# Four small moves in a one-layer hybrid decoder step: a weight cast, a norm's sum, the last pair's products, a row tile's store

## The chip, the cores and the metric

One core of one Trainium2 chip runs one decoder layer on a prompt of 512 tokens and eight samples of four tokens. The metric is the device time of one execution in microseconds (us); of several executions the median is taken. TensorE is called PE below, its weight loads PEld; VectorE is DVE, ScalarE is ACT, GpSimd is POOL, and SyncE, which only issues DMAs here, is SP.

## What is computed

The reference, cut to its frame (all in float32, model width 1024, 4096 feed-forward columns each for gate and value):

```python
def _layer(x, ...):
    m, ... = _mixer(_rmsnorm(x, norm_mix_pre), ...)      # recurrence + windowed attention, then @ w_out
    x = x + _rmsnorm(m, norm_mix_post)
    f, ffn_state = _conv_ffn(_rmsnorm(x, norm_ffn_pre), ffn_prev, w_up, ffn_conv_w, ffn_conv_b, w_down)
    x = x + _rmsnorm(f, norm_ffn_post)

def _mixer(h, ...):
    xr, q, k, v, g_lru, g_attn = split(h @ w_in)
    lru_out = rg_lru(causal_conv(xr, width 4))           # 8 block-diagonal gate groups
    attn = window_attention(q, k, v, window 128, 8 heads, 2 kv heads, sinks, relative bias)
    return (sigmoid(g_lru) * (lru_out @ w_lru_o) + sigmoid(g_attn) * (attn @ w_attn_o)) @ w_out

def _conv_ffn(h, prev, w_up, conv_w, conv_b, w_down):
    val, gate = split(causal_conv(h @ w_up, width 3))
    return (gelu(gate) * val) @ w_down
```

Outputs are the 512 prompt rows y_p, the 32 sample rows y_s, and the states of both groups.

## The kernel before

All 544 tokens (512 and 32) are handled together, with the model dimension on the partitions and tokens along the free side, in two halves of 272 (or 256 and 288 in the down projection). A float32 factor is split into a high part H (a rounded copy in the type fp32r, made by ACT or DVE: `wh_...`, `hH`, `fH`, `b21H`) and a low part L (the factor less its high part, a DVE or POOL subtraction: `wl_...`, `hL`, `fL`, `b21L`). Each product of factors is three matmuls: H by H, H by L and L by H, summed in PSUM.

The program runs through these stages: the first tiles of x are transposed and multiplied by a first weight; the input projection (`pmin`); recurrence and attention; their output projections (`pmlo`, `pmao`); w_out (`pmout`); the post norm, the residual x1 and the second pre norm; the up projection, in which pairs of columns (a gate column block and a value block, p_ = 0 to 31) are formed by seven products named a11, a12, p2, p3, p1, p4, a22 on sums and differences of four quarter operands b11, b21, b12, b22; tap (the width-3 convolution) and glu (gelu(gate) * value, split into fH and fL); the down projection (`pmdn`) in groups of four pairs, the last group (weights `wh_dl`, `wl_dl`) being kept to the end; the post norm; and the rows sent out.

PE runs in the order in which the program writes its instructions, in the whole kernel. ACT and DVE run in written order as well in the parts that the change touches, and SP in the last part. Work beside the products is written between them in steps: generators yield a number of steps, `later(k, f, ...)` puts f behind the next k steps. So a number in such a place sets where on PE, ACT and DVE an instruction stands.

Four places matter.

The start. `hsplit(k, ...)` splits one turned tile of x: ACT writes hH, DVE writes hL (`hL`, line 177). The loop of line 485 runs over z = 0, 1 (two halves of the model dimension) and k, four tiles each. Between them a weight half is cast to its high part by DVE (`wsplit_hi(..., eng=dve)`, line 285), and POOL subtracts for its low part (line 290). The matmuls `pm_first` follow, then the transposes of the other half of x (`ps_ta`, line 473).

The second norm. The function `norm_chain(a, ...)` sums the squares of x1 for half a. On DVE the partial squares are added into `accx`; then

```python
        yield NORM_TICKS[a]
        with tc.high_priority(offset=HP):
            r = stats(acc2, nch, f"f{a}")
            yield YS[a]
            dg = diag(r, n, f"f{a}")
        yield YB[a]
        with tc.high_priority(offset=HP):
            rep = spread(dg, n, f"f{a}")
```

`stats` is six small matmuls with ones (`pst_f`, half 1 at 446 us), then ACT's square root and DVE's Newton steps (`nst_f`); `diag` and `spread` put the result on all partitions by PE (`rep_f`). From there DVE makes the normalized tiles `h2t` and the operands b12 and b22. Meanwhile PE forms products of the operands b11 and b21, whose results are `pq_...` and are copied out to `ec`; their weights are `wh_e`, `wl_e`.

The last pair. For p_ = 31, a chain of tap and glu steps is laid between the last products (lines 1680 to 1685). glu 1 finishes `z` on DVE, glu 2 makes fH on ACT, glu 3 makes fL on DVE. On the same engines stand the splits of the last down weights (`wl_dl`) and the sums `ft += pmdn` which empty the down projection's PSUM tiles.

The tail. `rows_t(i)` turns row tile i back to rows (eight transposes `pyo`, two ACT copies into `yo`) and returns a function that issues its store. Row tiles 2 and 3 and the 32 sample rows leave like this; tiles 0 and 1 leave as `xtok`. `ends(z)` forms the last products of tile 1 (`pend`), `ends_square` their squares for the norm (ACT), `ends_gain` a DVE product, and `tokens_out` the result and its store.

Of the kernel before, what the change touches and what calls it, by code (L numbers as in the profile page):

```python
# [17 lines left out]
P = 128  # L18
# [35 lines left out]
APART = ()  # L54
DN_BUFS = 2
SUMS = (4, 3)
NORM_TICKS = (3.5, 1)
YS = (0.5, 0.5)
HP = 150
NSTART = (1, 0.5)  # L60
# [63 lines left out]
def hawk_step(ctx, tc, I, O):  # L124
    nc = tc.nc
    act, dve, pool, pe = nc.scalar, nc.vector, nc.gpsimd, nc.tensor
# [22 lines left out]
    def RAW(name):  # L149
        return rp.tile([P, D], F32, tag="raw", name=name)  # L150
# [4 lines left out]
    def PX(name):  # L155
        return psx.tile([P, 512], F32, tag="aux", name=name)
# [63 lines left out]
    ident = keep.tile([P, P], F32, name="ident")  # L220
# [50 lines left out]
    def wsplit_hi(un, eng=None):  # L271
        i, u = un // 2, un % 2
        hl = []
        for x in "hl":
            if order[i] in in_slots:
                t_ = S(f"w{x}{u}_{wname(i)}", F32R)[:, 0:512]
                t_ = t_.rearrange("p (k n) -> p k n", k=4)
            else:
                t_ = wp.tile([P, 4, P], F32R, tag="w", name=f"w{x}{u}_{wname(i)}")
            hl.append(t_)  # L280
        raw = wraw[i][:, 4 * u:4 * u + 4, :]
        if eng is None:
            act.activation(hl[0], raw, AF.Copy)  # L283
        else:
            eng.tensor_copy(hl[0], raw)
        wunits[un] = hl
        return raw, hl

    def wsplit_lo(raw, hl, eng=None):
        (eng or dve).tensor_tensor(out=hl[1], in0=raw, in1=f32(hl[0]), op=ALU.subtract)  # L290
# [78 lines left out]
    TOK = [(i * P, P, xp[i * P:(i + 1) * P, :]) for i in range(4)] + [(SEQ, NS, xs)]  # L369
# [82 lines left out]
    def hsplit(k, a, ps):  # L452
        g = pv[:, G_PRE + k:G_PRE + k + 1]
        act.activation(h.get(k, a, 0), ps, AF.Copy, scale=g)
        stt(h.get(k, a, 1), ps, g, f32(h.get(k, a, 0)), ALU.mult, ALU.subtract)
# [7 lines left out]
    def first_mm(k, i0, i1, start=False, stop=False):  # L463
        mm(first_ps[:, :256], wunits[k // 4][i0][:, k % 4, :], h.get(k, 0, i1), start, stop)
# [3 lines left out]
    def turn_a(z):  # L468
        for k in range(4 * z, 4 * z + 4):
            if not z:  # L470
                ps_ta.append(PX(f"ps_ta{k}"))
            for q in range(2):
                pe.transpose(turned_a(k)[:, q * P:(q + 1) * P], xtile(q, k), ident)

    def turned_a(k):
        return ps_ta[k % 4][:, k // 4 * 256:k // 4 * 256 + 256]

    def first_low(z):
        for k in range(4 * z, 4 * z + 4):
            first_mm(k, 1, 0, stop=k == KD - 1)  # L480
# [4 lines left out]
    for z in range(2):  # L485
        for k in range(4 * z, 4 * z + 4):
            hsplit(k, 0, turned_a(k))
            if k % 4 == 1 - z:
                raw, hl = wsplit_hi((u0, u1)[z], eng=dve)
                wsplit_lo(raw, hl, eng=pool)  # L490
        for k in range(4 * z, 4 * z + 4):
            first_mm(k, 0, 0, start=k == 0)
            if z and k > 4:
                first_mm(k - 1, 0, 1)
        if z == 0:
            turn_a(1)
            for k in range(4):
                first_mm(k, 0, 1)
            first_low(0)
# [733 lines left out]
    def norm_chain(a, acc):  # L1233
# [8 lines left out]
        with tc.high_priority(offset=HP):  # L1242
# [12 lines left out]
            for g in range(6 if a else 0):  # L1255
# [15 lines left out]
                yield 0.5  # L1271
        yield NORM_TICKS[a]
        with tc.high_priority(offset=HP):
# [246 lines left out]
    def product(ps, ws, nm, start, stop):  # L1520
        for k in range(4):
            wh, wl = (ws[j][:, k, :] for j in range(2))
            xh, xl = operand(nm, k, 0), operand(nm, k, 1)
            for i, (w, x) in enumerate(((wh, xh), (wh, xl), (wl, xh))):
                pe.matmul(ps[:, :HN], w, x, start=start and k == 0 and i == 0, stop=stop and k == 3 and i == 2,  # L1525
                          skip_group_check=True)
# [111 lines left out]
    def pair(p_, nm):  # L1638

        jv, jg = p_, 32 + p_  # L1640
        ps, e = pst.setdefault(p_, {}), e_.setdefault(p_, {})
        bank = {"a11": "x", "a12": "z", "p2": "x", "p3": "y", "p1": "x", "p4": "w" if p_ in apart else "x",
                "a22": "y"}[nm]
        start = bank not in ps
        if start:
            ps[bank] = PX(f"pu{bank}_{p_}")
        product(ps[bank], usplit["s", p_, nm], XOF[nm], start, nm in ("a12", "p4", "a22") or bank == "x" and nm == "p1" and p_ in apart)
        z = ps[bank][:, :HN]

        def taken(nm_):  # L1650

            e[nm_] = EP(f"{nm_}_{p_}")
            act.copy(e[nm_], z)  # L1653

        def u4_c22():
            taken("u4")
            ug = utile(jg)
            for o, y in zip(halves2(ug, ps["y"]), halves2(ug, e["u4"])):
                sub(o[0], o[1], y[1])

        def c11():
            add(utile(jv)[:, 2:2 + HN], e["e1"], z)

        def c12():
            if p_ in apart:
                for o, y in zip(halves2(ut[jv], z), halves2(ut[jv], e["u4"])):
                    add(o[0], y[1], o[1])
            else:
                for o in halves2(ut[jv], z):
                    act.copy(*o)  # L1670
            states(jg if p_ < 31 else jv)

        def c21():
            sub(ut[jg][:, 2:2 + HN], z, e["u2"])
            states(jv if p_ < 31 else jg)

        if nm in ("a11", "a12", "p2", "p1", "p4", "a22"):
            f = {"a11": lambda: taken("e1"), "a12": c11, "p2": lambda: taken("u2"), "p1": u4_c22, "p4": c12, "a22": c21}[nm]
            result(f)
        if p_ == 31 and nm in ("a22", "p4"):  # L1680
            j = jg if nm == "a22" else jv
            chain = [(1, tap, j, 0), (1 if j == jg else 2, tap, j, 1), (2, tap, j, 2)]
            chain += [(2, glu, p_, 0)] if j == jg else [(2, glu, p_, 1), (3, glu, p_, 2), (3, glu, p_, 3)]
            for k, f, *args in chain:
                later(k, f, *args)
        elif nm == "a22":
            for k, f, *args in ((1, tap, jv, 0), (2, tap, jv, 1), (2, tap, jg, 0), (3, tap, jv, 2), (4, tap, jg, 1),
                                (5, tap, jg, 2), (6, glu, p_, 0), (7, glu, p_, 1), (8, glu, p_, 2), (9, glu, p_, 3)):
                later(k + 3 if k >= 8 and p_ % CH == CH - 1 else k, f, *args)


    ft, xtok = {}, {}
# [74 lines left out]
    for i, x in enumerate(plan):  # L1767
# [7 lines left out]
        else:  # L1775
            _, q, c, a = x
# [6 lines left out]
    yp, ys = O["y_p"][0], O["y_s"].rearrange("b t d -> (b t) d")  # L1783
# [16 lines left out]
    def rows_t(i):  # L1800
        t0, nn, _ = TOK[i]
        dst = yp[t0:t0 + nn, :] if i < 4 else ys
        o = RAW(f"yo{i}")
        for kk in range(2):
            px = PX(f"pyo{i}_{kk}")
            for j in range(4):
                pe.transpose(px[:nn, j * P:(j + 1) * P], ft[4 * kk + j][:, t0:t0 + nn], ident)
            act.copy(o[:nn, kk * 512:(kk + 1) * 512], px[:nn, :])
        return lambda q=nc.sync: q.dma_start(out=dst, in_=o[:nn, :])

    sq7 = T("sq7")
    frow, fgs = {}, {}
# [55 lines left out]
    def ends(z):  # L1868
        ps = PM(f"pend{z}")
        o = ps[:, 0:256]  # L1870
        for k in range(CH):
            wh, wl = (usplit["dl", k, 1][j].rearrange("p k n -> p (k n)")[:, 256 * z:256 * z + 256]
                      for j in range(2))
            fh, fl = (F.t[QL * CH + k][j][:, P:2 * P] for j in range(2))
            pe.matmul(o, fh, wh, start=k == 0, stop=False, skip_group_check=True)
            if k == 0:
                for j in range(2):
                    pe.matmul(ps[:, j * P:(j + 1) * P], ft[4 + 2 * z + j][:, P:2 * P], ident, start=False, stop=False,
                              skip_group_check=True)
            pe.matmul(o, fl, wh, start=False, stop=False, skip_group_check=True)  # L1880
            pe.matmul(o, fh, wl, start=False, stop=k == CH - 1, skip_group_check=True)
        return o
# [43 lines left out]
    yo = [rows_t(2)]  # L1926
    o = ends(0)
# [2 lines left out]
    add(b_, ssq[:, 1, 0:1], ssq[:, 1, 1:2])  # L1930
    dve.tensor_scalar(b_, b_, 1.0 / D, EPS, ALU.mult, ALU.add)
    dve.tensor_scalar(h_, b_, -0.5, 0.0, ALU.mult, ALU.add)
    o = ends(1)
    ends_square(1, o)
    act.activation(s_, ssq[:, 1, 2:3], AF.Sqrt, scale=1.0 / D, bias=b_)
    ends_gain(1, o)
    yo += [rows_t(i) for i in (3, 4)]
    stt(v, ssq[:, 1, 2:3], -0.5 / D, h_, ALU.mult, ALU.add)
    dve.reciprocal(r, s_)
    stt(s_, r, r, v, ALU.mult, ALU.mult)  # L1940
    stt(r, s_, 1.5, r, ALU.add, ALU.mult)
    xo = [tokens_out(1, r, z) for z in range(2)]
    yo[2](act)
    for f in yo[:2] + xo:
        f()
    flush()
    order_.close()
# [32 lines left out]
```

## Time and profile before

| | |
|---|---|
| median of 3 runs | 991.08 us (990.84 to 991.33) |
| the profiled execution | 991.07 us, span of its instructions 989.3 us, granted clock 0.998 |
| PE busy | 979.6 us, 99% of the span, 7780 matmuls |
| DVE, ACT, POOL busy | 746.8, 558.3 and 160.9 us |
| DMA | 135.62 MB, mean 137 GB/s |
| the last transposes on PE | end at 982.8 us of the span |

A row of the timeline is: start, length, engine, line, operation, output <- inputs, shape, count (several like instructions in a row are put together), and in brackets the idle time ahead of it on its engine with what ended it. Matmuls are pipelined, so one's length is more than the distance to the next, which is about 0.12 to 0.13 us for 256 to 288 columns.

### The profile page before, as it was taken

To read this page: it belongs to the slowest core of one execution; us is meant where nothing else is said; L and a number is where in the kernel's file an instruction comes from. 1 tells how busy PE (TensorE), PEld (TensorE's weight loads), DVE (VectorE), ACT (ScalarE), POOL (GpSimd) and SP (SyncE) were. 2 spreads that over 40 slices of the span, in tenths; PEclk is the share of its full clock that TensorE was granted. 3 is DMA by queue.
4 is the path that set the end of the run, shared out by engine and by line. 5 is a ranking of instruction groups with operands and counts; after the bars stand their busy time and mean duration, and the time that the engine had idled before them with its cause. 6 is when DMAs were issued, how large, how long until landed. Compare 5 with 4: busy or idle time off the path is not lost.

```text
span 989.3 us, 20126 instructions
## 1 busy us (share of the span) xinstructions
PE 979.6 (99%) x7780; PEld 971.6 (98%) x7780; DVE 746.8 (75%) x1610; ACT 558.3 (56%) x1356; POOL 160.9 (16%) x271
## 2 busy tenths in 40 slices
PE   9999999999999999999999999999999999999997
PEld 8999999999999999999999999999999999999996
DVE  6777678766848555689786778787888888879866
ACT  6545334468476435556766665555655555556652
POOL 2143000002506341210011010101010101011004
PEclk9999999999999999999999999999999999999999
DMA  7675222323223535236058586867676767668612
GB/s 213 187 231 174 81 70 86 107 86 106 87 66 107 176 113 151 60 129 192 13 126 178 136 180 140 177 143 175 145 169 152 168 152 166 155 154 198 197 47 91
DMA packets 211111, 135.62 MB, mean 137 GB/s; under 512 B 8965, under 2 KB 197133, under 8 KB 210984
## 3 DMA queue, kind: packets, MB, share of 16 engines
q1 hardware_dynamic: 198984, 112.59, 40.0%
q0 software_dynamic: 11920, 19.59, 11.9%
q10 hardware_dynamic: 112, 2.17, 0.6%
q8 instruction: 61, 1.00, 0.4%
q14 instruction: 34, 0.28, 0.1%
HBM read 111.78 MB, written 11.37 MB: 124 GB/s over the span
## 4 chain that ended last, share of the span: by engine, by line
PE 96%; DVE 2%; ACT 1%; issue 0%; DVEq 0%; POOL 0%; ACTq 0%; POOLq 0%
PE pmin L165 22%; PE pmdn L165 17%; PE pux L1525 16%; PE puy L1525 8%; PE pq L1525 6%; PE pmout L165 5%; PE pmao L165 5%; PE pmlo L165 5%; PE puz L1525 4%; PE pg L165 1%; PE psc L165 1%; PE pvp L165 1%; PE ptok L165 1%; PE pt L819 1%; PE ps_warm L165 0%
## 5 line engine op out<-in xcount | busy, mean ns | idle before, releaser
L165 PE MATMUL pmin<-hH,wh_in 128*128 128x256 f32 (+1 forms) x568 | 164.6, 292 | 0.0
L165 PE MATMUL pmin<-hL,wh_in 128*128 128x256 f32 (+1 forms) x568 | 162.3, 288 | 0.0
L165 PE MATMUL pmin<-hH,wl_in 128*128 128x256 f32 (+1 forms) x568 | 159.0, 288 | 0.0
L165 PE MATMUL pmdn<-fH,wh_dn 128*128 128x256 f32 (+1 forms) x448 | 129.2, 288 | 0.0
L165 PE MATMUL pmdn<-fH,wl_dn 128*128 128x256 f32 (+1 forms) x448 | 129.2, 288 | 0.0
L165 PE MATMUL pmdn<-fL,wh_dn 128*128 128x256 f32 (+1 forms) x448 | 128.7, 287 | 0.0
L177 DVE SCALAR_TENSOR_TENSOR uc<-u,fv,uc 128x560 f32<-128x560 f32 x128 | 102.0, 797 | 11.6 <-ACT uc L1556 11.4
L165 PEld LDWEIGHTS pmin<-hH,wh_in 128*128 128x128 f32 x568 | 107.2, 189 | 1.4 <-issue 1.2
L165 PEld LDWEIGHTS pmin<-hL,wh_in 128*128 128x128 f32 x568 | 107.3, 189 | 0.1
L165 PEld LDWEIGHTS pmin<-hH,wl_in 128*128 128x128 f32 x568 | 104.7, 188 | 0.2 <-issue 0.2
L165 PEld LDWEIGHTS pmdn<-fL,wh_dn 128*128 128x128 f32 x448 | 84.4, 188 | 0.0
L165 PEld LDWEIGHTS pmdn<-fH,wl_dn 128*128 128x128 f32 x448 | 84.3, 188 | 0.0
L165 PEld LDWEIGHTS pmdn<-fH,wh_dn 128*128 128x128 f32 x448 | 84.3, 188 | 0.0
L1653 ACT COPY u<-pux 128x272 f32<-128x272 f32 x52 | 20.1, 386 | 84.3 <-PE pux L1525 84.2
L168 DVE TENSOR_TENSOR u<-puy,u 128x240 f32<-128x240 f32 (+2 forms) x78 | 24.7, 344 | 50.0 <-PE puy L1525 33.1
L283 ACT ACTIVATE wh_in<-raw_in 128x512 fp32r<-128x512 f32 x70 | 42.8, 628 | 30.9 <-issue 17.8
L174 DVE TENSOR_TENSOR ft<-ft,pmdn 128x256 f32<-128x256 f32 (+1 forms) x104 | 45.2, 436 | 17.1 <-PE pmdn L165 16.9
L290 DVE TENSOR_TENSOR wl_in<-raw_in,wh_in 128x512 fp32r<-128x512 f32 x70 | 48.0, 697 | 1.0 <-ACT wh_in L283 1.0
L1556 ACT ACTIVATE uc<-u,fv 128x560 f32<-128x560 f32 x64 | 48.3, 756 | 0.0
L1451 POOL DMA_DIRECT2D raw_up_s<-raw_up_s x26 | 22.7, 872 | 101.1 <-DMA raw_up_s<-raw_up__7493 4.6
L168 DVE TENSOR_TENSOR wl_dn<-raw_dn,wh_dn 128x512 fp32r<-128x512 f32 x56 | 38.3, 684 | 0.8 <-ACT wh_dn L1462 0.8
L776 ACT ACTIVATE s<-s,st 128x256 f32<-128x256 f32 (+1 forms) x32 | 15.2, 475 | 39.7 <-DVE st L773 26.9
(777 smaller groups left out, 3400.9 us busy)
## 6 DMA issues: line engine op xcount, KB each, us to landing
raw_in<-in_w_in_dram SPq DMA_DIRECT2D x35, 512.0 KB
raw_dn<-in_w_down_dram SPq DMA_DIRECT2D x56, 256.0 KB
raw_up_s<-in_w_up_dram SPq DMA_DIRECT2D x25, 512.0 KB
raw_up_s<-raw_up_s POOLq DMA_DIRECT2D x26, 256.0 KB, 5.5
raw_ao<-in_w_attn_o_dram SPq DMA_DIRECT2D x8, 512.0 KB
raw_lo<-in_w_lru_o_dram SPq DMA_DIRECT2D x8, 512.0 KB
raw_out<-in_w_out_dram SPq DMA_DIRECT2D x8, 512.0 KB
xdram<-xn POOLq DMA_DIRECT2D x8, 272.0 KB, 9.7
```

Source lines behind the costliest of these rows:

```text
L165: pe.matmul(out, l, r, start=start, stop=stop)
L168: dve.tensor_tensor(out=out, in0=a, in1=b, op=ALU.subtract)
L174: dve.tensor_tensor(out=out, in0=a, in1=b, op=ALU.add)
L177: dve.scalar_tensor_tensor(out=out, in0=a, scalar=s_, in1=b, op0=op0, op1=op1)
L283: act.activation(hl[0], raw, AF.Copy)
L290: (eng or dve).tensor_tensor(out=hl[1], in0=raw, in1=f32(hl[0]), op=ALU.subtract)
L776: act.activation(s3[:, j, :], s3[:, j, :], AF.Exp, bias=ng[:, j:j + 1], accum_out=sm[:, j:j + 1])
L819: pe.transpose(pt[:, (2 * ch + j) * P:(2 * ch + j + 1) * P], s3[:, j, ch * P:(ch + 1) * P], ident)
L1451: pool.dma_start(out=w["p4"], in_=w["p2"], accum_op=ALU.add)
L1525: pe.matmul(ps[:, :HN], w, x, start=start and k == 0 and i == 0, stop=stop and k == 3 and i == 2, skip_group_check=True)
L1556: act.activation(yt[j][:, 0:FLATU], u[:, 0:FLATU], AF.Copy, scale=fv[:, j:j + 1])
L1653: act.copy(e[nm_], z)
```

## The change

Four edits; no instruction is added or taken away except that one store becomes two. The diff, cut to its core:

```diff
-NORM_TICKS = (3.5, 1)
+NORM_TICKS = (3.5, 1.5)
...
             hsplit(k, 0, turned_a(k))
-            if k % 4 == 1 - z:
+            if k % 4 == 0:
                 raw, hl = wsplit_hi((u0, u1)[z], eng=dve)
                 wsplit_lo(raw, hl, eng=pool)
...
-            chain += [(2, glu, p_, 0)] if j == jg else [(2, glu, p_, 1), (3, glu, p_, 2), (3, glu, p_, 3)]
+            chain += [(2, glu, p_, 0)] if j == jg else [(3, glu, p_, 1), (4, glu, p_, 2), (4, glu, p_, 3)]
...
         for kk in range(2):
-            ...
+            rows_half(i, kk, o)
         return lambda q=nc.sync: q.dma_start(out=dst, in_=o[:nn, :])
+
+    def rows_half(i, kk, o):
+        t0, nn, _ = TOK[i]
+        w = slice(kk * 512, (kk + 1) * 512)
+        px = PX(f"pyo{i}_{kk}")
+        for j in range(4):
+            pe.transpose(px[:nn, j * P:(j + 1) * P], ft[4 * kk + j][:, t0:t0 + nn], ident)
+        act.copy(o[:nn, w], px[:nn, :])
+        return lambda: nc.sync.dma_start(out=yp[t0:t0 + nn, w], in_=o[:nn, w])
...
+    o3 = RAW("yo3")
+    yo.append(rows_half(3, 0, o3))
     o = ends(1)
     ends_square(1, o)
     act.activation(s_, ssq[:, 1, 2:3], AF.Sqrt, scale=1.0 / D, bias=b_)
     ends_gain(1, o)
-    yo += [rows_t(i) for i in (3, 4)]
+    yo += [rows_half(3, 1, o3), rows_t(4)]
...
-    yo[2](act)
-    for f in yo[:2] + xo:
+    yo[3](act)
+    for f in yo[:3] + xo:
```

At the start, the cast of the first weight half stands one hL sooner on DVE (for z = 1 nothing moves).

On DVE around the second norm's sum, before (numbers behind names count tiles; raw_up__5794 and raw_up__5859 are the weights of the two products that follow on b21 and then on b11):

```order
L168 TENSOR_TENSOR wl_e_1_6097<-raw_up__5711,wh_e_1_6096 128x512
L168 TENSOR_TENSOR wl_e_0_6117<-raw_up__5794,wh_e_0_6116 128x512
L168 TENSOR_TENSOR wl_e_0_6136<-raw_up__5859,wh_e_0_6135 128x512
L419 TENSOR_SCALAR nst_f_6155<-pst_f_6151 128x3
L420 RECIPROCAL nst_f_6155<-nst_f_6155 128x3
L171 TENSOR_TENSOR nst_f_6155<-nst_f_6155 128x3
L177 SCALAR_TENSOR_TENSOR nst_f_6155<-nst_f_6155 128x3 x2
L168 TENSOR_TENSOR wl_e_1_6165<-raw_up__5794,wh_e_1_6164 128x512
L1166 TENSOR_SCALAR dg_f_6182<-ident,nst_f_6155 128x128 x2
L1166 TENSOR_SCALAR dg_f_6182<-ident,nst_f_6155 128x16
L168 TENSOR_TENSOR wl_e_1_6187<-raw_up__5859,wh_e_1_6186 128x512
```

and now:

```order
L168 TENSOR_TENSOR wl_e_1_6097<-raw_up__5711,wh_e_1_6096 128x512
L168 TENSOR_TENSOR wl_e_0_6117<-raw_up__5794,wh_e_0_6116 128x512
L168 TENSOR_TENSOR wl_e_0_6136<-raw_up__5859,wh_e_0_6135 128x512
L168 TENSOR_TENSOR wl_e_1_6154<-raw_up__5794,wh_e_1_6153 128x512
L419 TENSOR_SCALAR nst_f_6175<-pst_f_6171 128x3
L420 RECIPROCAL nst_f_6175<-nst_f_6175 128x3
L171 TENSOR_TENSOR nst_f_6175<-nst_f_6175 128x3
L177 SCALAR_TENSOR_TENSOR nst_f_6175<-nst_f_6175 128x3 x2
L168 TENSOR_TENSOR wl_e_1_6183<-raw_up__5859,wh_e_1_6182 128x512
L1166 TENSOR_SCALAR dg_f_6200<-ident,nst_f_6175 128x128 x2
L1166 TENSOR_SCALAR dg_f_6200<-ident,nst_f_6175 128x16
```

The Newton steps stand behind one more weight split, and the last of these splits ahead of `dg_f`. On PE the six `pst_f` stand behind the twelve matmuls of the product pq_34 on b21 instead of ahead of them, and `rep_f` behind the product pq_35 on b11.

On DVE in the last pair, before (`pmdn_4_1`, `pmdn_5_1`, `pmdn_6_1` are down-projection tiles of the second token half):

```order
L177 SCALAR_TENSOR_TENSOR uc_13055<-u_12889,fv,uc_13055 128x560 x2
L177 SCALAR_TENSOR_TENSOR z_13073<-uc_13055,fv,uc_12994 128x512
L177 SCALAR_TENSOR_TENSOR z_13073<-uc_13055,fv,uc_12994 128x32
L174 TENSOR_TENSOR ft_7362<-ft_7362,pmdn_4_1_13057 128x288
L168 TENSOR_TENSOR fL_13094<-z_13073,fH_13093 128x544
L168 TENSOR_TENSOR wl_dl_0_13077<-raw_dl_12801,wh_dl_0_13076 128x512
L168 TENSOR_TENSOR wl_dl_0_13098<-raw_dl_12826,wh_dl_0_13097 128x512
L174 TENSOR_TENSOR ft_7468<-ft_7468,pmdn_5_1_13079 128x288
L168 TENSOR_TENSOR wl_dl_0_13102<-raw_dl_12849,wh_dl_0_13101 128x512
```

and now:

```order
L177 SCALAR_TENSOR_TENSOR uc_13055<-u_12889,fv,uc_13055 128x560 x2
L174 TENSOR_TENSOR ft_7362<-ft_7362,pmdn_4_1_13057 128x288
L177 SCALAR_TENSOR_TENSOR z_13090<-uc_13055,fv,uc_12994 128x512
L177 SCALAR_TENSOR_TENSOR z_13090<-uc_13055,fv,uc_12994 128x32
L168 TENSOR_TENSOR wl_dl_0_13074<-raw_dl_12801,wh_dl_0_13073 128x512
L168 TENSOR_TENSOR wl_dl_0_13094<-raw_dl_12826,wh_dl_0_13093 128x512
L174 TENSOR_TENSOR ft_7468<-ft_7468,pmdn_5_1_13076 128x288
L168 TENSOR_TENSOR fL_13116<-z_13090,fH_13115 128x544
L168 TENSOR_TENSOR wl_dl_0_13098<-raw_dl_12849,wh_dl_0_13097 128x512
```

The first ft sum stands ahead of z, and the first two weight splits and the second ft sum ahead of fL.

On SP at the end of the program, the difference (yo tiles are rows of tile 2 and 3, xtok of tile 1; the line numbers shift by the new function):

```order
-L1893 DMA out_dram<-xtok_1_13216 128x512
-L1809 DMA out_dram<-yo_13524 128x1024
-L1809 DMA out_dram<-yo_13577 128x1024
-L1893 DMA out_dram<-xtok_0_13253 128x512
-L1893 DMA out_dram<-xtok_1_13286 128x512
+L1899 DMA out_dram<-xtok_1_13216 128x512
+L1806 DMA out_dram<-yo_13524 128x1024
+L1815 DMA out_dram<-yo_13558 128x512 x2
+L1899 DMA out_dram<-xtok_0_13253 128x512
+L1899 DMA out_dram<-xtok_1_13286 128x512
```

Row tile 3 is stored in two halves. On PE the four transposes of its first half stand between the products of ends(0) and ends(1) instead of behind both; on ACT its copy stands ahead of the last square.

More of the change, by code (lines that the diff above doesn't have):

```diff
@@ L1804, in rows_t @@
         for kk in range(2):
[L1805 to L1808, printed above, removed]
+            rows_half(i, kk, o)
         return lambda q=nc.sync: q.dma_start(out=dst, in_=o[:nn, :])
+    def rows_half(i, kk, o):
[6 more added lines that the diff above has]
+        return lambda: nc.sync.dma_start(out=yp[t0:t0 + nn, w], in_=o[:nn, w])
     sq7 = T("sq7")
```

## Prediction

> **What bounds the kernel now.** I read the chain of waits of the page first. This is its share by engine:
>
> ```profile
> PE 96%; DVE 2%; ACT 1%; issue 0%; DVEq 0%; POOL 0%; ACTq 0%; POOLq 0%
> ```
>
> The end is set by TensorE (PE) nearly everywhere, so the next view is what PE waited for, over the whole span. Columns: the waiting tile and line, what ended the wait, then total us, times and the longest.
>
> ```profile
> core 0 of [0], span 989.3 us
> PE pm_first L165 <- DVE wh_in L285: 1.1, 1, 1.1
> PE ps_warm L165 <- POOL ones L219: 1.0, 1, 1.0
> PE pmdn L165 <- DVE ft L174: 0.6, 1, 0.6
> PE pst_f L165 <- DVE accx L174: 0.3, 1, 0.3
> ```
>
> Four waits, 3.0 us together, are all there is to win on PE short of removing matmuls, and the change removes none. Three of its edits stand at three of these waits; the fourth stands in the tail, where PE has ended. Because PE has no other wait, a gain at 7 us is handed on to the end unless one of the later waits eats it. A measurement of this kernel can tell about 0.2%, here 1.98 us, from no change, so the whole question is whether the four terms add up to that. The sum is made against the profiled execution, 991.07 (span 989.3 and 1.77 around it), which lies 0.01 under the median of the runs.
>
> **Edit A, the first weight's cast one step sooner.** DVE at the start, and then PE (start, length, in us):
>
> ```profile
> 6.31 0.88 DVE L177 SCALAR_TENSOR_TENSOR hL<-ps_ta,pv,hH 128x256 fp32r<-128x256 f32 x2 [0.78 <-ACT hH L454]
> 7.10 0.42 DVE L285 CAST wh_in<-raw_in 128x512 fp32r<-128x512 f32 x1
> ```
>
> ```profile
> 7.67 0.71 PE L165 MATMUL pm_first<-hH,wh_in 128*128 128x256 f32 x4 [1.06 <-DVE wh_in L285]
> 8.21 0.93 PE L473 MATMUL ps_ta<-ident,x 128*128 128x128 f32 x7
> ```
>
> Two hL take 6.31 to 7.10, so one is 0.395. The cast moves ahead of one of them; PE's first matmul goes from 7.67 to about 7.28. What is late next are the transposes of the second halves of x at 8.21: they would start near 7.8, and need data that no row shows waiting. If that data lands by 7.8 the gain is 0.39; if it lands at 8.2 it is 0. The hL that the cast passes is late by 0.4, but PE reads hL only behind those eight transposes. A loss is excluded, since nothing that PE needs before 8.21 is moved later. I take 0.3, nearer the full end, because the row at 8.21 carries no wait. The POOL subtraction behind the cast moves sooner with it.
>
> **Edit B, the second norm's sum half a step later.** Before, DVE and PE around it:
>
> ```profile
> 444.36 1.94 DVE L174 TENSOR_TENSOR accx<-accx,sq_x 128x272 f32<-128x272 f32 x4
> 446.21 0.69 DVE L168 TENSOR_TENSOR wl_e<-raw_up__5711,wh_e 128x512 fp32r<-128x512 f32 x1
> ```
>
> ```profile
> 446.35 0.83 PE L165 MATMUL pst_f<-ones,accx 128*128 128x1 f32 x6 [0.34 <-DVE accx L174]
> 447.04 0.37 PE L1525 MATMUL pq<-b21H,wh_e 128*128 128x272 f32 x1
> ...
> 448.63 0.29 PE L1525 MATMUL pq<-b11H,wh_e 128*128 128x272 f32 x1
> ```
>
> The sums pst_f now stand behind the twelve matmuls of the product at 447.04. Those no longer wait for accx. But their third operand is the low part wl_e that DVE splits directly behind accx, ended at 446.90, and DVE's order there is unchanged. So PE would begin the product at 446.0 or sooner (446.35 less the wait of 0.34), do two matmuls, and stand until about 446.97. Ten more at 0.13 (twelve take 447.04 to 448.63) bring 448.27; pst_f costs 446.35 to 447.04, 0.69, now behind it: 448.96, against 448.63 before. **The wait is not removed, it changes its name from accx to wl_e and grows**: a loss of 0.33, say 0.3.
>
> What comes out of pst_f comes later too. ACT's square root, DVE's Newton steps behind it, and the next split:
>
> ```profile
> 447.22 0.26 ACT L418 ACTIVATE nst_f<-pst_f,epst 128x3 f32<-128x3 f32 x1 [2.15 <-PE pst_f L165]
> 448.02 0.15 DVE L419 TENSOR_SCALAR nst_f<-pst_f 128x3 f32<-128x3 f32 x1
> ...
> 448.77 0.68 DVE L168 TENSOR_TENSOR wl_e<-raw_up__5794,wh_e 128x512 fp32r<-128x512 f32 x1
> ```
>
> After, pst_f starts at 448.27; ACT follows 0.87 behind as before (446.35 to 447.22), ends at 449.40; DVE's steps take 0.75 (448.02 to 448.77), and the wl_e of the second b11 product, still queued behind them, takes 0.68 from 450.15 to 450.83. PE has the first b11 product from 448.93, twelve matmuls, and wants that wl_e at the third of the second, 450.75: 0.15 more with 0.07 to notice it. Last, the replicated norm rep_f is now behind this product, near 452.2, and its users follow:
>
> ```profile
> 450.87 1.73 DVE L177 SCALAR_TENSOR_TENSOR h2t<-x,pv,rep_f 128x272 f32<-128x272 f32 x4 [0.29 <-issue]
> 455.42 1.53 DVE L168 TENSOR_TENSOR b22L<-h2t,b22H 128x544 fp32r<-128x544 f32 x2
> L1525 PE MATMUL pq<-b22L,wh_e x4: 287/288/292, 457.6 to 458.8; 128*128 128x272 f32 x4
> ```
>
> DVE is at these rows almost without a gap. h2t began at 450.87, at the earliest about 0.7 behind rep_f; now near 452.9, 2.0 later. The two b22L ended near 456.2 and 456.95 and are wanted at 457.6 and two thirds of the group later, 458.4: margin 1.4, with PE's own 0.45 lateness 1.9. So 0.05 to 0.1 more, with 0.5 as its upper end. B costs 0.3 + 0.15 + 0.05 = 0.5, between 0.25 and 0.9. The preparation of the next operands half a step later, and one exchange on SP's queue (a weight load behind one more u copy), have no PE wait near them in the list above; I cost them nothing, since that list shows every operand there in time, and 0.3 more if the next operands have no margin.
>
> **Edit C, the last pair's gated products a step later.** DVE, and then PE:
>
> ```profile
> 940.97 0.91 DVE L177 SCALAR_TENSOR_TENSOR z<-uc,fv,uc 128x512 f32<-128x512 f32 x2
> 941.80 0.45 DVE L174 TENSOR_TENSOR ft<-ft,pmdn 128x288 f32<-128x288 f32 x1
> 942.61 0.73 DVE L168 TENSOR_TENSOR fL<-z,fH 128x544 fp32r<-128x544 f32 x1 [0.36 <-ACT fH L1575]
> 943.25 1.29 DVE L168 TENSOR_TENSOR wl_dl<-raw_dl,wh_dl 128x512 fp32r<-128x512 f32 x2
> 944.45 0.45 DVE L174 TENSOR_TENSOR ft<-ft,pmdn 128x288 f32<-128x288 f32 x1
> 944.82 1.29 DVE L168 TENSOR_TENSOR wl_dl<-raw_dl,wh_dl 128x512 fp32r<-128x512 f32 x2
> ```
>
> ```profile
> 944.12 0.29 PE L165 MATMUL pmdn<-fH,wl_dn 128*128 128x288 f32 x1
> 945.04 0.38 PE L165 MATMUL pmdn<-fH,wh_dl 128*128 128x288 f32 x1 [0.63 <-DVE ft L174]
> ```
>
> PE's matmul at 945.04 waits for the second ft sum, which empties a PSUM bank. It could start at 944.25, one pitch of 0.13 behind 944.12: 0.79 late, and its first row is 0.09 longer than the others, so 0.87 in all. After: ft takes z's place at 940.97 and holds DVE for 0.37 (944.45 to 944.82), z for 0.83, to 942.17; two wl_dl for 1.2 (943.25 to 944.45), to 943.37; the second ft ends at 943.8. The bank is free 0.4 before PE wants it. What is late next: fL follows (0.64, to 944.4) and behind it the last two wl_dl, ready near 945.05 and 945.65. PE, now begun at 944.25, wants them nine and twelve pitches in, near 945.3 and 945.7: margins of 0.25 and 0.05 to 0.1. fH and fL are first wanted by the tenth and eleventh matmul, near 945.4 and 945.55, an us behind. So C gains 0.87, and 0.7 if the thin margin is missed by 0.17.
>
> **Edit D, half of row tile 3 sent sooner.** The stores on SP's queue; then, by stretch, the bytes of all queues (last column, GB/s):
>
> ```profile
> 978.59 2.03 SPq L1893 DMA_DIRECT2D out_dram<-xtok  x2
> 980.71 2.55 SPq L1809 DMA_DIRECT2D out_dram<-yo  x2
> 983.53 1.04 SPq L1893 DMA_DIRECT2D out_dram<-xtok  x2
> ```
>
> ```profile
> 979.30:980.00 0.70, 0.70 (x8) 0.70 (x8) 0.70 (x1) 0.70 (x3) 0.40 (x1) 1.00 0.82 310
> 981.00:983.00 2.00, 1.77 (x17) 1.40 (x15) 1.22 (x7) 1.83 (x6) 0.00 (x0) 1.00 0.97 381
> 983.00:983.60 0.60, 0.00 (x0) 0.00 (x0) 0.60 (x2) 0.60 (x2) 0.00 (x0) 1.00 0.12 41
> 983.60:987.80 4.20, 0.00 (x0) 0.00 (x0) 0.56 (x1) 0.23 (x1) 0.00 (x0) 0.70 0.84 281
> 987.80:989.30 1.50, 0.00 (x0) 0.00 (x0) 0.00 (x0) 0.00 (x0) 0.00 (x0) 0.50 0.00 0
> ```
>
> From 983.6 on 1.18 MB drain at 281 GB/s: tile 3 (0.52 MB), two xtok (0.26 each), the sample rows (0.13). Then come 1.5 us without a byte. After, 0.26 MB of tile 3 are ready by 981 and fall into the idle stretch 983.0 to 983.6 behind the bytes of tile 2. The drain is shorter by 0.26 MB / 281 GB/s = 0.93. The price: four transposes (0.11 each by the seven at 8.21) now stand ahead of the last products, so the final sum of squares and the xtok stores are 0.44 later: issues at about 983.97 and 984.63. A single 256 KB store, the first row at 978.59, has moved 0.22 MB of its 0.26 by 980.0 (0.7 at 310 GB/s) and is done near 980.3, 1.7 behind its issue. So the last xtok ends no earlier than 986.3, and the most D can win is 987.75 − 986.3 = 1.45. With 0.93 as the middle bound and 1.45 as the upper, I take 1.2; the lower end is −0.44, where the late xtok alone decide.
>
> The two stores issued back to back ran at 381 GB/s in 981 to 983, so I charge no fixed time for the extra one. The Trainium skill speaks against the split: DMA: Bandwidth & Descriptors fits a DMA issued from GpSimd as 2.0 us fixed plus its bytes at 436 GB/s (Anatomy of one DMA) and asks for 1 MiB or more in each (Bandwidth). By it one 512 KB store (estimate 3.2) made into two (2.6 each) loses 2.0, with the transposes D is −2.4 and the time 992.8. That fit is for GpSimd's path, and these stores come from SP.
>
> **The sum:** 0.3 − 0.5 + 0.87 + 1.2 = 1.87, so 991.07 − 1.87 = **989.2**, on the edge of the 1.98 that can be told.
>
> **The rivals.**
> *The tail follows the xtok stores (14%).* If the bytes were not what is late, D is −0.44. The gain is 0.3 − 0.5 + 0.87 − 0.44 = 0.23, time 990.8, no change. For it: SP issues the last xtok only after 984; against: 4.2 us at a mean of 281 GB/s behind 983.6, so bytes and not issues are what is late.
> *B does what it says (12%).* The wait of 0.34 goes and nothing takes its place: 1.87 + 0.5 + 0.34 = 2.7, time 988.4, faster. For it: the tile that PE's wait names is accx alone; against: the wl_e directly behind accx on DVE.
> *The extra store is served in series (8%).* Place: SP's queue behind tile 2. The half store alone takes 1.7 from issue to last byte (as at 978.59), and 1.5 lie between the last byte and the end. If each store must finish before the next one's bytes flow, the split adds 3.2 and sheds 0.93 of tile 3's: 2.27, and with 0.44 for the transposes D is −2.7: 0.67 − 2.71 = −2.04, time 993.1, slower. It decides once the extra store costs over 2.2 (0.67 − 0.44 − 2.2 = −1.97). Against: the 381 GB/s of 981 to 983, where one store's end and the next one's beginning leave no gap. The Trainium skill's fixed 2.0 us (DMA: Bandwidth & Descriptors, Anatomy of one DMA), read as serial, speaks for it.
>
> **How the numbers follow.** The forecast has 66%; its own range is 988.6 (A 0.39, B 0.25, D 1.45) to 990.1 (A 0, B 0.7, D 0.8). Some three fifths of it, 0.38, lie beyond the bound at 989.1 or so: D's middle is held down by a bound of bytes that the rate of 381 GB/s would loosen, and B's terms of 0.15 and 0.05 are the least sure. With the 0.12 of the second rival that makes faster 0.50; the rest of the forecast (0.28) and the first rival (0.14) are 0.42 for same; slower 0.08. The range reaches to the first and second rival, 988.3 to 990.8, and leaves out the third and the tails of the others.
>
> **What would show it.** A: PE's wait for wh_in at 0.65 to 0.75, the second transposes before 8.0. B: the wait for accx gone, one for wl_e of 0.9 to 1.1 in its place and a small one in the second b11 product; the time between the product ahead of pst_f and the b22 products 0.5 longer. C: no wait for ft near 944; the dl products begin 0.13 behind the dn ones. D: two 128x512 stores on SP, bytes between 983.0 and 983.6, and from the last matmul to the end 1.6 less than before (1.2, and 0.44 of matmuls that moved ahead of it). What proves me wrong: b22 no later against the first b21 product (B), or as long from the last matmul to the end as before (D).

## The result, and the profile after

The changed kernel takes 993.47 us (median of 14 runs, 992.95 to 995.02) against 990.99 before (990.68 to 992.18): a ratio of 1.0024, 95% interval 1.0016 to 1.0032. It is 2.5 us slower, and outside the predicted range of 988.3 to 990.8. The profiled execution took 993.1 with a span of 991.3, 2.0 more than before.

PE's waits after the change, over the whole span:

```profile
core 0 of [0], span 991.3 us
PE pq L1525 <- DVE wl_q L168: 1.8, 3, 1.1
PE ps_warm L165 <- POOL ones L219: 1.0, 1, 1.0
PE pq L1525 <- DVE h2t L177: 1.0, 1, 1.0
PE pq L1525 <- DVE wl_e L168: 0.7, 1, 0.7
PE pm_first L165 <- DVE wh_in L285: 0.3, 1, 0.3
```

The waits for ft and accx are gone, that for wh_in has shrunk, and three new ones, 3.5 us together, stand in the up projection's products pq. All three come behind the place of edit B. Here are their rows on PE, of which the last three lie 50 to 63 us behind the first:

```profile
446.78 0.40 PE L1525 MATMUL pq<-b21H,wl_e 128*128 128x272 f32 x1 [0.68 <-DVE wl_e L168]
...
457.31 0.37 PE L1525 MATMUL pq<-b12H,wh_e 128*128 128x272 f32 x1 [0.99 <-DVE h2t L177]
...
497.12 0.40 PE L1525 MATMUL pq<-b21H,wl_q 128*128 128x272 f32 x1 [0.22 <-DVE wl_q L168]
505.46 0.39 PE L1525 MATMUL pq<-b11H,wl_q 128*128 128x272 f32 x1 [0.39 <-DVE wl_q L168]
509.87 0.40 PE L1525 MATMUL pq<-b21H,wl_q 128*128 128x272 f32 x1 [1.14 <-DVE wl_q L168]
```

Lined up row by row, PE's stream is 0.18 us ahead of the one before up to edit B, 0.17 behind at 455, 1.40 behind at the first b12 product, 1.9 at 498 and 3.88 at 510. From there to 890 it drifts back to 3.2 without a wait there in the list of either trace; I found no cause for that. In the last pair it falls to 2.33, and over the tail to 2.0. So B cost 4.06 up to 510 and 3.4 net of the drift, C gave 0.86 and D 0.37. The drift comes with B: it is there in the trace of B alone (3.96 behind at 510, 3.27 at 940), and not in that of C alone.

**The b12 wait.** DVE's first four and last two h2t after, and then the last two of before:

```profile
452.53 1.72 DVE L177 SCALAR_TENSOR_TENSOR h2t<-x,pv,rep_f 128x272 f32<-128x272 f32 x4 [1.35 <-issue]
456.26 0.90 DVE L177 SCALAR_TENSOR_TENSOR h2t<-x,pv,rep_f 128x272 f32<-128x272 f32 x2
```

```profile
454.61 0.90 DVE L177 SCALAR_TENSOR_TENSOR h2t<-x,pv,rep_f 128x272 f32<-128x272 f32 x2
```

The first b12 product starts at 457.31, just when the last two h2t have ended (457.16). Those are not its operands (they belong to b22; the last of its own, the low part b12L, ended at 456.35), but they are the last to read rep_f in PSUM. That the product needs the PSUM buffer which rep_f held is the likeliest reading of the name in the bracket; it is argued, not shown. Before, the last h2t ended at 455.51 and this product started at 455.91: a margin of 0.4, not the 1.4 that I took from b22L.

**The waits for wl_q.** ACT and DVE ahead of the wait at 497, before and then after:

```profile
487.43 1.20 ACT L1304 ACTIVATE t1H<-h2f 128x544 fp32r<-128x544 f32 x2
489.73 0.77 ACT L1567 ACTIVATE uc<-uc,fv 128x560 f32<-128x560 f32 x1 [0.84 <-DVE u L1532]
492.27 0.75 ACT L1556 ACTIVATE uc<-u,fv 128x560 f32<-128x560 f32 x1
```

```profile
493.05 0.81 DVE L177 SCALAR_TENSOR_TENSOR uc<-u,fv,uc 128x560 f32<-128x560 f32 x1 [0.33 <-ACT uc L1556]
493.77 0.69 DVE L168 TENSOR_TENSOR wl_q<-raw_up__6070,wh_q 128x512 fp32r<-128x512 f32 x1
```

```profile
491.25 0.76 ACT L1567 ACTIVATE uc<-uc,fv 128x560 f32<-128x560 f32 x1 [2.70 <-DVE u L1532]
492.44 1.19 ACT L1304 ACTIVATE t1H<-h2f 128x544 fp32r<-128x544 f32 x2
494.87 0.75 ACT L1556 ACTIVATE uc<-u,fv 128x560 f32<-128x560 f32 x1
```

```profile
495.66 0.80 DVE L177 SCALAR_TENSOR_TENSOR uc<-u,fv,uc 128x560 f32<-128x560 f32 x1 [2.69 <-ACT uc L1556]
496.38 0.69 DVE L168 TENSOR_TENSOR wl_q<-raw_up__6070,wh_q 128x512 fp32r<-128x512 f32 x1
```

Here ACT and DVE hand the convolution uc to each other. Before, the two t1H (1.2 us of ACT) stood ahead of an idle time of ACT and cost nothing. Half a step later they stand behind it: ACT first waits 2.70 for DVE, then does t1H, and DVE waits 2.69 for ACT's uc. The split wl_q, queued on DVE behind that uc, slips from 493.77 to 496.38, and PE waits for it at 497.12.

The longest of these waits, 1.14 at 509.87, falls on a wl_q for which PE had no room before either. The split on DVE before and after, and PE's rows before:

```profile
505.25 0.68 DVE L168 TENSOR_TENSOR wl_q<-raw_up__6162,wh_q 128x512 fp32r<-128x512 f32 x1
509.13 0.68 DVE L168 TENSOR_TENSOR wl_q<-raw_up__6151,wh_q 128x512 fp32r<-128x512 f32 x1
```

```profile
505.67 0.28 PE L1525 MATMUL pq<-b21L,wh_q 128*128 128x272 f32 x1
505.99 0.40 PE L1525 MATMUL pq<-b21H,wl_q 128*128 128x272 f32 x1
```

Here PE starts 0.32 behind the row ahead, where 0.13 is usual, just when wl_q has ended (505.93), and the row is longer than its neighbours. That is a stall of about 0.3, but the row ahead ends at 505.95, so the view counts 0.04 of idle time and its list of waits does not name it.

**Edit C** did what was forecast. The first matmul of the last group (weights wh_dl) stands one pitch of 0.13 behind the last one of the group before (weights wl_dn):

```profile
947.33 0.29 PE L165 MATMUL pmdn<-fH,wl_dn 128*128 128x288 f32 x1
947.46 0.29 PE L165 MATMUL pmdn<-fH,wh_dl 128*128 128x288 f32 x1
```

**The tail.** SP's stores after, and the bytes of its last stretch:

```profile
983.10 0.38 SPq L1806 DMA_DIRECT2D out_dram<-yo  x1
983.58 2.03 SPq L1815 DMA_DIRECT2D out_dram<-yo  x2
986.36 1.00 SPq L1899 DMA_DIRECT2D out_dram<-xtok  x2
```

```profile
986.90:989.70 2.80, 0.00 (x0) 0.00 (x0) 0.10 (x1) 0.00 (x0) 0.00 (x0) 0.94 0.84 235
989.70:991.30 1.60, 0.00 (x0) 0.00 (x0) 0.00 (x0) 0.00 (x0) 0.00 (x0) 0.50 0.00 0
```

PE's last transposes end at 985.17, so the tail behind PE is 6.13 us (6.53 before). From there to the first xtok store it is 1.19 (0.76 before: the 0.44 of the four transposes), and from there to the end 4.94 (5.77 before).

### The profile page after: what moved, and what is told of

The parts are those of the page before. It is cut to its first block, busy times and chain, and to the rows that moved or that the text cites. A ratio compares the mean times of both kernels' runs of the same rounds, so it can differ in the third digit from the quotient of the medians.

```text
span 991.3 us, 20131 instructions
## 1 busy us (share of the span) xinstructions
PE 980.4 (99%) x7780; PEld 971.5 (98%) x7780; DVE 746.6 (75%) x1610; ACT 558.0 (56%) x1356; POOL 160.9 (16%) x271
## 4 chain that ended last, share of the span: by engine, by line
PE 92%; DVE 3%; ACT 2%; DMA 1%; issue 1%; SPq 0%; DVEq 0%; ACTq 0%
PE pmin L165 22%; PE pmdn L165 18%; PE pux L1525 16%; PE puy L1525 8%; PE pmout L165 5%; PE pmao L165 5%; PE pmlo L165 5%; PE puz L1525 4%; PE pq L1525 2%; PE pg L165 1%; PE psc L165 1%; DVE uc L177 1%; PE pvp L165 1%; PE ptok L165 1%; PE pt L819 1%
```

## The experiments

Each is timed in five rounds against the kernel before, which ran at 990.9 to 991.2.

**B alone.**

```diff
-NORM_TICKS = (3.5, 1)
+NORM_TICKS = (3.5, 1.5)
```

> Edit B alone (the second norm's sum half a step later). Theory 1, read from the two traces: B alone makes the loss, and it comes in three places: about 0.35 us where PE waits for wl_e, about 1.2 where the first b12 product waits for h2t, and about 2.5 between 495 and 510 us where PE waits for wl_q, 4.1 in all: some 4 us slower than before. Rival: the loss needs the other edits too (A brings PE forward into waits, C or D add some): B alone then costs 0.5 to 1.5.

994.33 against 991.06, ratio 1.0035 (1.0023 to 1.0048): 3.3 us slower, with the same three waits as in the whole change. The loss is B's own, and less than the 4 expected, since the drift behind 510 gives back 0.7.

**The change without B.** `NORM_TICKS` back to (3.5, 1).

> The changed kernel with B taken back (A, C and D stay). Theory 1: faster than before by A 0.2, C 0.86 and D 0.4, so 1.4 to 1.5 us, with PE's waits for ft and accx: ft gone, accx still 0.3. Rival (the tail D costs, or the three interact): 0.9 or less.

989.83 against 991.06, ratio 0.9989 (0.9981 to 0.9998): 1.2 faster, between the two forecasts; the wait for ft is gone and that for accx still 0.3.

**D alone.**

> Edit D alone. Theory 1, from the tail of the changed kernel's trace (6.53 us from the last transposes to the end before, 6.13 after, on PE work of the same length): 0.4 us faster than before. The prediction's own theory, bytes bound: 1.2 faster. Rival, the late xtok stores decide: 0.4 slower.

990.73 against 991.06, ratio 0.9998 (0.9989 to 1.0007): 0.3 faster by the medians, which the interval does not tell from nothing. Its tail behind PE is 6.17 us, as after.

**B with the later splits in their old slots.**

```diff
-NORM_TICKS = (3.5, 1)
+NORM_TICKS = (3.5, 1.5)
-TX = 4
+TX = 3.5
```

> B alone, but the wait ahead of the splits of t3, t1 and t4 is half a step shorter (TX 3.5 for 4), so that these stand on ACT and DVE where they stood before. It tells where the last 2.5 us of B's loss come from. Theory 1a, the place in the queues: the waits for wl_q at 497 to 510 go, and B then costs 0.35 + 1.2 = 1.6. Theory 1b, the lateness of h2t is carried on by ACT and DVE: it still costs about 4.

992.16 against 991.06, ratio 1.0012 (1.0003 to 1.0021): 1.1 slower. PE's waits for h2t and wl_e are there, those for wl_q are gone:

```profile
PE pq L1525 <- DVE h2t L177: 1.0, 1, 1.0
PE pq L1525 <- DVE wl_e L168: 0.7, 1, 0.7
```

So the last part of the loss is a matter of place in the queues of ACT and DVE. (TX is the pause ahead of the splits of t3, t1 and t4, sums and differences of the quarter operands.)

**The later splits alone, half a step later.** `TX = 4.5`, nothing else.

> The kernel before with only TX raised from 4 to 4.5: the norm's sum, rep_f, h2t and the splits of b12 and b22 stay where they were, and only the splits of t3, t1 and t4 stand half a step later on ACT and DVE. If their place in the queues is what cost 2.2 us in B: waits for wl_q (or t3, t1) of 1 to 2.5 us appear between 490 and 510 although nothing was late, and it is 1 to 2.5 us slower than before. If a late h2t is needed for it as well: within 0.3 of before.

993.72 against 991.01, ratio 1.0027 (1.0017 to 1.0036): 2.7 slower, though the norm was in time. The wait is there, and neither h2t nor wl_e is waited for:

```profile
PE pq L1525 <- DVE wl_q L168: 2.5, 3, 1.1
```

The place alone makes it, and costs a little more than the 1 to 2.5 expected.

**B with the half step taken off behind the sum.** `YB = (0.5, 0)` with B.

> B with the half step given back behind the sum (YB 0 for 0.5): pst_f stands half a step later as in B, but rep_f and everything behind it stand in their old places. By the theory that rep_f's place, not pst_f's, makes the b12 wait: the wait for h2t and those for wl_q go; PE waits 0.7 for wl_e and now 0.7 to 1.0 for dg_f at rep_f; 1.0 to 1.3 slower than before. By the theory that pst_f's lateness makes it: over 3 slower.

994.56 against 991.01, ratio 1.0032 (1.0019 to 1.0044). The edit did not do what I wrote: a pause of 0 put rep_f a whole product later, to 453.5, and not back to its old place. The wait at the first b12 product grew to 1.9 (now named after ACT's copy ec), so it fits that rep_f's place makes this wait, but it does not separate rep_f from pst_f. The next one does.

**rep_f alone later.**

```diff
-YB = (0.5, 0.5)
+YB = (0.5, 1)
-TX = 4
+TX = 3.5
```

> The kernel before with rep_f alone moved: behind the first b11 half of pq_35 as in B, while pst_f stays ahead of pq_34 and the splits of t3, t1, t4 stay in their old slots (YB 1 for 0.5, TX 3.5 for 4). If the 1.2 us at the first b12 product come from rep_f's place on PE: a wait for h2t of about 1, 1.0 to 1.3 us slower than before, no wait for wl_e, the one for accx as before. If they come from pst_f's lateness: within 0.2 of before.

991.77 against 991.12, ratio 1.0006 (0.9997 to 1.0015). By the medians 0.65 slower, less than expected, and the interval takes in none as well as 1.5. The trace is clear about the wait: 1.0 for h2t with pst_f in its old place, none for wl_e, and the b12 product at 457.24 (455.91 before). Lined up row by row, PE stands 1.24 later there; 0.3 of it comes back at 506, where before PE stood for wl_q, and 0.2 more by 975.

**A alone.**

> Edit A alone. By the offset of PE's matmuls in the changed kernel's trace (0.39 sooner at the first product, 0.06 to 0.18 sooner from the next stage on): 0.1 to 0.2 faster than before, about what five rounds can tell. The prediction's 0.3 to 0.39 if the second halves of x land sooner in most runs.

991.09 against 991.12, ratio 0.9999 (0.9990 to 1.0008): nothing that can be told from none. PE's rows:

```profile
6.71 0.70 PE L165 MATMUL pm_first<-hH,wh_in 128*128 128x256 f32 x4 [0.69 <-DVE wh_in L285]
7.38 0.33 PE L473 MATMUL ps_ta<-ident,x 128*128 128x128 f32 x1
8.04 0.98 PE L473 MATMUL ps_ta<-ident,x 128*128 128x128 f32 x7 [0.33 <-DMA x<-in_x_prompt_dram]
```

The wait for the cast is 0.37 shorter, and PE then waits 0.33 for x. One trace says little here, since in the traces without A this wait goes from 0.29 to 1.11. Over all of them it comes out the same: in the eight traces without A the first product starts at 7.67 by the median, in the eleven with A at 7.28; but the product behind the second transposes starts at 9.01 and at 8.94. So the cast gains 0.39, and 0.07 of it is left behind the transposes.

**C alone.**

> Edit C alone: the wait for ft gone, PE's offset to before 0.87 smaller from 945 us on: 0.87 us faster than before. Rival, the last two wl_dl are late instead: 0.5 or less, with a wait for wl_dl near 945.

990.11 against 991.15, ratio 0.9990 (0.9981 to 0.9999): 1.0 faster, the wait for ft gone and none for wl_dl.

**What sets the tail: without the second half of tile 3, and without the sample rows.** Two kernels with A, C and D, each without one store.

> A, C and D without the store of the second half of row tile 3 (left out: 512 of the 1024 columns of 128 rows of y_p are not written; everything else is). It tells what sets the tail behind D. If bytes do (the prediction's theory): 0.26 MB less at 250 to 290 GB/s, 0.9 to 1.0 us faster than the version with A, C and D, so near 988.9. If the chain to the last xtok store and that store's own time do: no more than 0.3 faster.

> A, C and D without the store of the 32 sample rows (left out: y_s is not written). Leaving out the half of tile 3 changed nothing, so what makes the last xtok store take 2.6 us from issue to last byte instead of the 1.7 of one alone may be the store on ACT's queue beside it. If so: 0.3 to 0.8 faster than A, C and D. If the xtok store takes this time by itself: within 0.2 of it.

Without the half tile 989.75 (ratio 0.9989, 0.9980 to 0.9998): the same as with it. Without the sample rows 988.94 (0.9978, 0.9969 to 0.9987): 0.9 faster than A, C and D. Bytes by the microsecond (last column), A, C and D without the half tile:

```profile
983.00:984.00 1.00, 0.00 (x0) 0.00 (x0) 0.47 (x1) 0.00 (x0) 0.00 (x0) 1.00 0.66 111
984.00:985.00 1.00, 0.00 (x0) 0.00 (x0) 0.00 (x0) 0.00 (x0) 0.00 (x0) 1.00 0.75 221
985.00:986.00 1.00, 0.00 (x0) 0.00 (x0) 0.00 (x0) 0.00 (x0) 0.00 (x0) 1.00 0.88 303
```

A quarter megabyte less is moved, and the end stays where it was; the DMA engines are busy for 0.66 of the first stretch with 111 GB/s. So behind D the bytes of tile 3 are not what is late. From the end of the last xtok issue to the end of the span it takes 3.9 with A, C and D and 2.9 without the sample rows (the issues end at 983.74 and 984.75 by the spans' own clocks, the spans at 987.7 and 987.6): the small store on ACT's queue holds up the large one beside it.

**The order of the last stores.** First, both xtok stores ahead of the second half of tile 3:

> A, C and D with SP's last stores in another order: both xtok stores ahead of the second half of tile 3. If bytes set the tail: the same as A, C and D (989.8) within 0.2, or up to 0.6 slower because nothing is moved while SP waits for xtok. If the last xtok store is late because it shares the DMA engines with the half tile ahead of it: 0.3 to 0.6 faster.

990.34 against 991.01 (0.9993, 0.9984 to 1.0002), 0.5 slower than A, C and D: the half tile is now the last. Then the sample rows sooner, in three ways: first of all behind ends(1) on SP's queue, the same on ACT's queue (both with all of tile 3's transposes behind ends(1)), and ahead of the second half with D as it is.

> A and C, tile 3 in two halves, all its transposes behind ends(1), and the sample rows turned and copied first and stored by SP ahead of the halves of tile 3, instead of last and on ACT's queue. If the sample rows' store beside the last xtok store is what made that store take 2.6 us: 0.4 to 0.9 faster than with the store late (989.44), near 988.7. If what counts is only how many bytes are still to move: within 0.2 of 989.44.

> As the one before, but the sample rows stay on ACT's queue, issued right behind their two copies and ahead of tile 3's copies. If the early place alone helps: as that one, less the 0.4 us by which ACT's issue holds up the copies of tile 3, which are not what is late. If the two queues side by side are the trouble: slower than it by 0.3 or more.

> A, C and D as they are, but the sample rows are turned and copied ahead of the second half of tile 3 and stored by SP ahead of it. The last xtok stores then have neither the sample rows beside them nor more than a half tile ahead. If the sample rows' late store is what D left over: 0.3 to 0.8 faster than A, C and D (989.83) and the fastest of all. If SP's issue of one more store in front of xtok eats it: within 0.2 of 989.83.

989.77 (0.9987, 0.9978 to 0.9995), 990.08 (0.9991, 0.9982 to 1.0000) and 989.54 (0.9986, 0.9977 to 0.9995). None wins the 0.9: by the medians the first two are slower than the 989.44 that they were to beat (the version of the next paragraphs), and the last, though 0.3 faster than A, C and D, is not told from it by the intervals. With the sample rows first, SP cannot issue xtok before 983.24, though DVE has finished the first at about 982.4: it is queued behind the halves of tile 3. Part of why this store is dear can be read from the last of the three, where it runs on SP's queue with no other store beside it. Rows of 128 partitions first, then the sample rows, which lie on 32:

```profile
982.00:983.00 1.00, 0.34 (x4) 0.10 (x1) 0.84 (x6) 1.00 (x3) 0.00 (x0) 1.00 0.98 383
983.75:984.25 0.50, 0.00 (x0) 0.00 (x0) 0.42 (x1) 0.00 (x0) 0.00 (x0) 1.00 1.02 221
```

The DMA engines are busy all the time in both, and move 383 and 221 GB/s. So the sample rows take more of the engines' time than their 0.13 MB say, on SP's queue too. Why their rate is lower, and whether another place for them is cheaper, stays open.

**The split without the move on PE.** A and C, tile 3 in two halves, all transposes behind ends(1):

```diff
-    o3 = RAW("yo3")
-    yo.append(rows_half(3, 0, o3))
     o = ends(1)
...
-    yo += [rows_half(3, 1, o3), rows_t(4)]
+    o3 = RAW("yo3")
+    yo += [rows_half(3, 0, o3), rows_half(3, 1, o3), rows_t(4)]
```

> A and C, with row tile 3 stored in two halves but all its transposes behind ends(1) as before. If the chain from the last products to the xtok store sets the tail, it starts 0.44 sooner here than in D, and the half tile that is now late is free as the other half was: 0.2 to 0.4 faster than A, C and D, near 989.5. If the bytes ahead of xtok count: 0.2 to 0.6 slower than it, 990.0 to 990.4.

> The same kernel as split_late, on the same chip as the one beside it, to compare the two: 989.4 within 0.2.

989.44 against 991.12 (0.9983, 0.9974 to 0.9992), and a second time 989.45 against 990.88 (0.9986, 0.9977 to 0.9995). It is the fastest of the versions that store everything, 1.4 to 1.7 us faster than before; the 0.4 that it has on A, C and D, and the 0.1 on the last of the three above, lie within the width of the intervals. Its tail behind PE is 5.83 us, against 6.53 before and 6.13 with the whole change.

## Why the prediction was wrong

**A**: forecast 0.3, measured none (the interval is 0.9 us to either side). The step that failed is "the row at 8.21 carries no wait": a row that would have to wait 0.1 us later shows none either. The lower end, data landing at 8.2, is what the traces show: the cast gains 0.39 and the transposes leave 0.07 of it.

**B**: forecast 0.5 lost, measured 3.3. Its first step held: the wait changed its name from accx to wl_e, 0.68 in the trace, and the b11 product came 0.3 later. The 0.15 at the second b11 product did not show: there is no second wait for wl_e. Two steps failed. First, "margin 1.4" was the margin of b22L's own readers; a tighter row was the b12 product's, 0.4 behind the last h2t. The h2t came 1.65 later (455.51 to 457.16), and PE went from 0.17 to 1.40 behind there. Second, "have no PE wait near them in the list above; I cost them nothing": the list shows what waits now and says nothing of the room, and it even left out a stall of 0.3 for a wl_q at 506. Moving the splits of t3, t1 and t4 alone by half a step cost 2.7 us.

**C**: forecast 0.87; 0.86 in the trace, 1.0 alone. Right in its size and its steps.

**D**: forecast 1.2; 0.33 alone, 0.37 in the trace's tail. The term was mis-sized by its own price: the drain from the first xtok issue to the end fell by 0.83 (forecast 0.93), but the 0.44 of the transposes, which I worked out and left out of this middle bound, had to be taken from it: 0.83 less 0.44 is 0.39. The step "bytes and not issues are what is late" does not hold behind D either, since half a tile less changed nothing; there the rival of the xtok stores names rightly what is late, though not its price of 0.44 lost.

Of the rivals, none held the loss. The one on the slower side, the extra store served in series, stood in the tail, while the loss was in B; that its time of 993.1 lies near the measured 993.47 is chance. The Trainium skill's fixed cost of each DMA, which it fits for DMAs issued from GpSimd (DMA: Bandwidth & Descriptors, Anatomy of one DMA), did not decide here: the split into two stores, without the move on PE, is in the fastest version that stores everything. No run shows the split alone.

## What to carry to other kernels

When a written order on two engines that hand work to each other is shifted, list every instruction behind the shift up to the next place where an engine has slack, and price it by the idle time of its own engine ahead of it, not by the waits of the engine that sets the end. Where matmuls overlap, look for a start that comes late behind the row ahead as well; the list of waits can miss it. A margin is taken at the first reader on the critical engine, and for every buffer that it needs, not only for its operands. What is put ahead of the last chain is paid there, even where the work itself is free: here 0.44 of the 0.83 that the split gave.

## What the runs showed of the hardware

The store of the 32 sample rows (0.13 MB, beside xtok's on another queue) cost 0.9 us at the end, where half a row tile (0.26 MB) ahead on the same queue cost none. Alone on SP's queue the sample rows, on 32 partitions, moved at 221 GB/s with the DMA engines busy throughout; rows on 128 partitions moved at 383 GB/s.
